# A scheduler that prices occupancy and latency apart, a gate whose left operands are turned by VectorE and by transfers, and operand tiles in three rooms

## The chip, the cores and the metric

The kernel runs on one core of one Trainium2 chip. A core has five engines with instruction queues of their own: TensorE (PE in the profile; its weight loads are PEld), VectorE (DVE), ScalarE (ACT), GpSimd (POOL) and SyncE (SP), which here only starts transfers. They meet through semaphores. The metric is the device time of one execution in microseconds (us). The time before is the median of three runs, 806.38 us, with 805.48 the lowest and 808.88 the highest.

## The reference, cut to what matters

One layer of a streaming encoder trunk is computed for 1024 prompt rows and 32 sample rows of width 1024, in float32:

```python
hn = rmsnorm(h, g_pre)
qA, kA, vA, gA, qB, kB, vB, gB = split(hn @ w_in)          # w_in: 1024 x 4096
oA = band_attention(qA, kA, vA)       # 8 heads x 64, own chunk of 64 and 8 before, biases
oB = stick_breaking(qB, kB, vB)       # 8 heads x 64, log-sigmoids and a reverse cumulative sum
y  = concat(oA * silu(gA), oB * silu(gB)) @ w_out           # 1024 x 1024
h  = h + rmsnorm(y, g_post)                                 # called h1 here
h  = h + sigmoid(h @ w_ple_gate) * (p @ w_ple)              # gate: 1024 x 1024
```

The outputs are h and the key and value caches. The change concerns the passage from the last line but one to the last: h1 stands with its rows on the partitions after the norm, and the gate's matmul wants it with its columns on the partitions.

## The kernel before, in words

**How precision is kept.** A float32 operand is split into a high part in a short float type (F32R) and a low remainder; a product is three matmuls, high by high, high by low and low by high (`multiply`, L1568). The high part is a ScalarE cast, the low part a VectorE subtraction.

**Stages.** From 0 to about 50 us the input rows are normed and turned and the first projections run. From 50 to about 550 us eight pairs of heads of the two attentions run, with the next pairs' input projections between them; about 550 to 605 us are the last input projection, 605 to 622 us the products `ple` of p. From 622 to 705 us runs the output projection ("o" in the names), from 705 to 801 us the gate projection ("g"), and the rest is the tail.

**The two last projections.** Both are Strassen-Winograd products over tiles of 128 rows. There are four sets: o with row tiles (0,4) and (1,5), o with (2,6) and (3,7), then g with the same two. A pair inside a set is an upper tile t and a lower tile t+4. Each set runs seven products in the order P1, P2, P6, P7, P4, P5, P3, and each product is 12 matmuls of 128x512 for each of the two pairs. In the profile the pair's products write tiles `o0P`, `o1P`, `g0P` and so on, after the upper row tile. The left operands A11, A12, S2, S3, A22, S1, S4 are made by `Side.make` (L1547) two or three products ahead (`AHEAD`): a ScalarE copy into PSUM, a ScalarE cast to the high part (`whA11o`, or a part of `A11o0`), a VectorE subtraction for the low part, and for some a GpSimd or VectorE combination before. `Side.room` gives them their places: pair 0 rotates over three rooms, two in the pool `fb` and one in `fa`, both tagged "ao"; pair 1 has `wpool` tiles. The short ninth tile (32 sample rows) has operands from `short_left` (L1642) and products from `short_product` (L1666); for the gate they are called `x8g`, `xb8g` and `g8`, and run after the third set.

**The gate's input.** `Row.close` (L1597) takes the mean square of a finished row tile, scales it by VectorE into `h1`, adds x by GpSimd and stores h1 to memory (`h_dr`). `Side.load` (L1530) makes the two operand tiles of a pair, `u` for tile t in pool `at2` and `l` for tile t+4 in pool `at0` or `fa`, and calls `fetch_T` (L1507) for each. For o it loads turned rows straight from memory. For g it loads the 128 rows of h1 in one transfer (`ht`), turns them by eight TensorE transposes into two PSUM banks (`pth`), and copies the banks to SBUF by two ScalarE copies (`ug`, `lg`). It does so for nine tiles. `Side.load` for the next set's pair is called when the last operand (n equal to 6) of this set's pair is made.

**What sets the order.** The body only records operations. `Recorder.order` (L372) is a list scheduler: each engine has a planned time at which it is free, an operation has a planned time at which its inputs are ready, and among the ready ones of an engine that with the smallest key goes first. The key is a class and the position in the program; `rec.low`, which is -2 or -1 around some row work, stands ahead of the position for the engines other than TensorE. `cost` (L338) gives two numbers: `busy`, how long the engine is taken, and `late`, how much later the result is there. In the kernel before only TensorE and the transfers have a `late` above 0. An operation on another engine is ready 60 ns after that (`SEM`), 460 ns if it is on TensorE (`MARGIN`); one on the same engine, when the engine is free. `emit` then issues all operations in the order found, each queue in turn, so the order is fixed before the kernel runs and every operation carries the line of `emit`, L450 in the profile. Instructions on a queue never pass each other. SP's queue holds all transfers.

Of the kernel before, what the change touches and what calls it, by code (L numbers as in the profile page):

```python
# [263 lines left out]
class Recorder:  # L264
# [73 lines left out]
    def cost(eng, method, args, kw, writes, reads):  # L338
# [8 lines left out]
        if eng == "ACT":  # L347
            return (165 if psum else 200) + 0.83 * n + (190 if "accum_out" in kw else 0), 0
        if eng == "DVE":
            if method == "tensor_tensor_scan":  # L350
                return 155 + 2.08 * n, 0
            if method == "tensor_copy" and not psum:
                return 155 + 0.53 * n, 0
            if method == "scalar_tensor_tensor":
                return 210 + 1.04 * n, 0
            return 155 + 1.04 * n + (83 if method == "tensor_tensor_reduce" else 0), 0
        if eng == "POOL":
            if method == "tensor_tensor":
                if n == 1:
                    return 400, 0  # L360
                return 190 + (1.77 if out.buf.dtype == F32 else 2.15) * n, 0
# [10 lines left out]
    def order(self):  # L372
# [17 lines left out]
        while len(out) < len(self.ops):  # L390
# [37 lines left out]
            for u in users[id(o)]:  # L428
                if u.eng == e and e != "SP":
                    r = t if e == "CTL" else free[e]  # L430
# [25 lines left out]
def stream_step(  # L456
# [1050 lines left out]
    def fetch_T(src, dst, t):  # L1507
# [5 lines left out]
        t0, n = rows_of(t)  # L1513
        h = fa.tile([P, D], F32, tag="hh", name=f"ht{t}", bufs=2)
        dma(h[0:n], h1_dr[t0:t0 + n, :])
        for q in range(2):
            pt = psum("T", f"pth{t}_{q}")
            for k in range(4):
                nc.tensor.transpose(pt[:, k * P:k * P + n], h[0:n, (q * 4 + k) * P:(q * 4 + k + 1) * P], ident[0:n, 0:n])
            nc.scalar.copy(dst[:, 4 * q:4 * q + 4, 0:n], pt.rearrange("p (k t) -> p k t", k=4)[:, :, 0:n])  # L1520


    class Side:
# [6 lines left out]
        def load(self):  # L1530
            self.u = at2.tile([P, KD, P], F32, tag="tok", name=f"u{self.nm}", bufs=2)
            if self.first:
                self.l = fa.tile([P, KD, P], F32, tag="hh", name=f"l{self.nm}", bufs=2)
            else:
                self.l = at0.tile([P, KD, P], F32, tag=("kd0", "kl0")[self.pair], name=f"l{self.nm}")
# [3 lines left out]
        def room(self, n, key):  # L1539
            if self.pair == 0:  # L1540
                one = Side.taken % 3 == 2
# [4 lines left out]

        def make(self, n, s2):  # L1547
            key = LEFT[ORDER[n]]
            u1, u2, l1, l2 = self.u[:, 0:4], self.u[:, 4:8], self.l[:, 0:4], self.l[:, 4:8]
# [7 lines left out]
            hi, lo = self.room(n, key)  # L1557
            beside = psum("mm" if self.m == 3 or (self.m == 2 and n > 1) else "T", f"x{key}{self.nm}").rearrange("p (k t) -> p k t", k=KT)
# [308 lines left out]
```

## Time and profile before

| | |
|---|---|
| median of the runs | 806.38 us (805.48 to 808.88, three runs) |
| the profiled execution, its own time | 808.3 us |
| its span, first to last instruction | 806.5 us |
| mean granted TensorE clock | 0.996 |
| TensorE busy in the span | 784.5 us, 97% |
| VectorE, ScalarE, GpSimd busy | 575.5, 507.8, 436.8 us |
| TensorE matmul records | 4646 |
| data moved by transfers | 161.08 MB |

The profile is of one execution; the 808.3 us are its time, 1.8 us longer than its span. A group line names an engine, an operation, the tile written and the tiles read, with the number of instructions. A waits line names what an engine waited for: the tile of the waiting instruction, the engine and the tile of what ended the wait, then the time in all, the number of waits and the longest one in us. A timeline line begins with the time in the span and the length in us; x12 means that twelve like instructions are drawn together, and the bracket at the end gives a wait before it. A windows line gives the stretch, its length, the busy time of PE, PEld, DVE, ACT and POOL with their counts, the granted clock, the transfers' share and GB/s. A tile answer gives line, engine, operation and tiles, the count, then the shortest, mean and longest duration in ns, the first and last start in us, and the shapes.

### The profile page before, as it was taken

To read this page: it belongs to the slowest core of one execution; us is meant where nothing else is said; L and a number is where in the kernel's file an instruction comes from. 1 tells how busy PE (TensorE), PEld (TensorE's weight loads), DVE (VectorE), ACT (ScalarE), POOL (GpSimd) and SP (SyncE) were. 2 spreads that over 40 slices of the span, in tenths; PEclk is the share of its full clock that TensorE was granted. 3 is DMA by queue.
4 is the path that set the end of the run, shared out by engine and by line. 5 is a ranking of instruction groups with operands and counts; after the bars stand their busy time and mean duration, and the time that the engine had idled before them with its cause. 6 is when DMAs were issued, how large, how long until landed. Compare 5 with 4: busy or idle time off the path is not lost.

```text
span 806.5 us, 14268 instructions
## 1 busy us (share of the span) xinstructions
PE 784.5 (97%) x4646; PEld 722.4 (90%) x4646; DVE 575.5 (71%) x1007; ACT 507.8 (63%) x1063; POOL 436.8 (54%) x503
## 2 busy tenths in 40 slices
PE   8999999999999999999999999999998999999997
PEld 6899989999889998999999989999996877888786
DVE  6627678886588897778896878766355687586565
ACT  5636675676476655785666685543337867876741
POOL 5613656873556676234660336777541537699523
PEclk9999999999999999999999999999999999999999
DMA  8419987668877749745545667774579767659743
GB/s 275 152 38 276 232 247 243 168 181 237 229 210 228 203 147 272 190 137 152 125 115 159 153 171 231 218 211 151 156 236 329 245 188 231 216 179 343 249 137 131
DMA packets 160971, 161.08 MB, mean 200 GB/s; under 512 B 39153, under 2 KB 120793, under 8 KB 160898
## 3 DMA queue, kind: packets, MB, share of 16 engines
q1 hardware_dynamic: 160898, 160.18, 67.0%
q8 instruction: 37, 0.61, 0.3%
q14 instruction: 36, 0.29, 0.1%
HBM read 99.23 MB, written 52.49 MB: 188 GB/s over the span
## 4 chain that ended last, share of the span: by engine, by line
PE 84%; ACT 5%; POOL 3%; DVE 3%; DMA 2%; issue 2%; SPq 1%; DVEq 0%; ACTq 0%; POOLq 0%
PE mm_gB L450 6%; PE mm_gA L450 6%; PE mm_qA L450 5%; PE mm_kA L450 5%; PE mm_vA L450 5%; PE mm_qB L450 4%; PE mm_kB L450 4%; PE SB L450 4%; PE PVB L450 4%; PE mm_vB L450 3%; PE PVA L450 3%; PE SA L450 3%; PE ptwB L450 3%; PE o0P L450 3%; PE o1P L450 2%; PE g0P L450 2%
## 5 line engine op out<-in xcount | busy, mean ns | idle before, releaser
L450 DVE TENSOR_TENSOR_SCAN om<-om,SB 128x384 f32<-128x384 f32 (+5 forms) x96 | 95.6, 1005 | 12.1 <-ACT om L450 9.8
L450 POOL TENSOR_TENSOR be<-om 128x128 f32<-128x128 f32 (+7 forms) x64 | 77.5, 1216 | 49.4 <-DVE om L450 23.1
L450 ACT ACTIVATE om<-SB 128x384 f32<-128x384 f32 (+5 forms) x96 | 44.9, 494 | 29.9 <-DVE SB L450 17.7
L450 ACT ACTIVATE be<-om,statA 128x640 f32<-128x640 f32 (+3 forms) x64 | 44.5, 696 | 12.1 <-DVE statA L450 6.9
L450 ACT CAST wTh<-ptwB 128x512 fp32r<-128x512 f32 (+3 forms) x64 | 29.4, 482 | 21.1 <-PE ptwB L450 16.2
L450 DVE TENSOR_TENSOR wTl<-be,wTh 128x640 fp32r<-128x640 f32 (+1 forms) x32 | 35.5, 1108 | 7.1 <-ACT wTh L450 6.8
L450 DVE TENSOR_TENSOR wTl<-ptwB,wTh 128x512 fp32r<-128x512 f32 (+3 forms) x64 | 33.5, 545 | 7.7 <-ACT wTh L450 4.6
L450 DVE TENSOR_TENSOR wTl<-ptwA,wTh 128x512 fp32r<-128x512 f32 (+2 forms) x64 | 29.8, 482 | 11.6 <-ACT wTh L450 10.1
L450 PE MATMUL SB<-kdB,LB 128*128 128x384 f32 (+5 forms) x96 | 33.7, 354 | 1.9 <-DVE om L450 1.9
L450 DVE CUSTOM_DVE_ANT_0 om<-SA,biasA 128x320 f32<-128x320 f32 (+3 forms) x64 | 30.0, 483 | 6.2 <-PE SA L450 5.8
L450 PE MATMUL SB<-klB,LB 128*128 128x384 f32 (+5 forms) x96 | 32.9, 347 | 0.0
L450 DVE STREAM_TRANSPOSE om<-be 128x640 f32<-128x640 f32 (+1 forms) x32 | 28.8, 900 | 4.7 <-ACT be L450 2.3
L450 ACT CAST wTh<-ptwA 128x512 fp32r<-128x512 f32 (+2 forms) x64 | 26.1, 424 | 9.0 <-PE ptwA L450 8.2
L450 PE MATMUL SA<-kdA,LA 128*128 128x320 f32 (+2 forms) x96 | 30.0, 322 | 1.3 <-DVE LA L450 0.7
L450 POOL TENSOR_TENSOR sggA<-sggA,oggA 128x352 f32<-128x352 f32 x24 | 23.9, 997 | 13.6 <-DVE sggA L450 10.2
L450 POOL TENSOR_TENSOR oB<-oB,oB 128x256 f32<-128x256 f32 x32 | 24.4, 783 | 12.0 <-DMA oB<-in_w_out_dram 5.8
L450 PE MATMUL SA<-klA,LA 128*128 128x320 f32 (+2 forms) x96 | 29.3, 316 | 0.0
L450 PE MATMUL ptwB<-ident,be 128*128 128x128 f32 x192 | 29.3, 273 | 0.0
L450 ACT CAST wTh<-be 128x640 fp32r<-128x640 f32 (+1 forms) x32 | 24.9, 779 | 6.4 <-DMA be<-swapA 3.8
L450 PE MATMUL ptwA<-ident,be 128*128 128x128 f32 x160 | 26.8, 274 | 2.0 <-ACT be L450 1.3
L450 POOL TENSOR_TENSOR gB<-gB,gB 128x256 f32<-128x256 f32 x32 | 24.3, 783 | 4.7 <-DMA gB<-in_w_ple_gate_dram 4.3
L450 DVE TENSOR_TENSOR SB<-SB,maskb 128x128 f32<-128x128 f32 x64 | 17.6, 290 | 11.3 <-PE SB L450 11.1
(707 smaller groups left out, 2659.7 us busy)
## 6 DMA issues: line engine op xcount, KB each, us to landing
swapA<-om SPq DMA_DIRECT2D x16, 320.0 KB, 2.7
be<-swapA SPq DMA_DIRECT2D x64, 80.0 KB, 3.2
oB<-in_w_out_dram SPq DMA_DIRECT2D x16, 256.0 KB, 4.6
sum_dro<-oB SPq DMA_DIRECT2D x16, 256.0 KB, 3.8
gB<-in_w_ple_gate_dram SPq DMA_DIRECT2D x16, 256.0 KB, 4.2
sum_drg<-gB SPq DMA_DIRECT2D x16, 256.0 KB, 3.0
x<-in_x_prompt_dram SPq DMA_DIRECT2D x16, 256.0 KB, 4.0
h_dr<-h SPq DMA_DIRECT2D x8, 512.0 KB, 3.2
```

The costliest lines, as they stand in the source:

```text
L450: getattr(getattr(tc.nc, o.what[0]), o.what[1])(*args, **kw)
```

## The change

**The planner's prices.** For ScalarE, VectorE and GpSimd's tensor operations the one price becomes two: a smaller time for which the engine is taken and a time (105, 85 or 150, and 40 ns) by which the result comes later. An operation that needs a result of its own engine is now ready when that result is there and not when the engine is free, except on TensorE. No instruction changes by this; the order in which each queue gets them does.

**The gate's input rows.** `Row.close` has a new step: VectorE transposes the finished 128x1024 row tile in squares of 32x32 into a tile `hs` (one buffer in `fb`), and a transfer stores it to memory as `turned` (512 KB). The plain store to `h_dr` stays, as the gate's last addition reads it. `fetch_T` for the gate has no TensorE transposes, no PSUM banks and no copies any more: four transfers, one for each quarter of the columns, read 32 partitions each of `turned` and so put the squares where they belong. In the operand tile a column's 128 rows then lie in four runs of 32 elements, so the operations of `make` read through a `blocks` view that puts them in order. In all 72 transposes and 18 copies go, nine VectorE transposes, nine stores and 36 loads in place of nine come.

**The rooms.** The operand tiles `u` and `l` of a pair now come from one of three rooms in rotation, (2m + pair) mod 3: two buffers "tok" in `at2`, two "hh" in `fa`, or "kd0"/"kl0" in `at0`. A pair's tiles are loaded three pairs ahead (`wanted`, `load_sides`), as soon as the room's former pair is done with its operands and, for the gate, the two row tiles are turned. In `Side.room` the pool `fa` gives the first of every three places and not the third, so the very first operand `A11o0` has its place in `fa`.

```diff
@@ -345,20 +345,22 @@
                 return (109 if args[1].shape[0] > 64 else 62), 165
             return max(109.0, 2.5 + 0.449 * args[2].free()) * (1 if args[2].buf.dtype == F32R else 4), 165
         if eng == "ACT":
-            return (165 if psum else 200) + 0.83 * n + (190 if "accum_out" in kw else 0), 0
+            return (60 if psum else 95) + 0.83 * n + (190 if "accum_out" in kw else 0), 105
         if eng == "DVE":
             if method == "tensor_tensor_scan":
-                return 155 + 2.08 * n, 0
+                return 120 + 2.1 * n, 85
             if method == "tensor_copy" and not psum:
-                return 155 + 0.53 * n, 0
+                return 70 + 0.53 * n, 85
             if method == "scalar_tensor_tensor":
-                return 210 + 1.04 * n, 0
-            return 155 + 1.04 * n + (83 if method == "tensor_tensor_reduce" else 0), 0
+                return 125 + 1.04 * n, 85
+            if method == "tensor_tensor_reduce":
+                return 90 + 1.04 * n, 150
+            return 70 + 1.04 * n, 85
         if eng == "POOL":
             if method == "tensor_tensor":
                 if n == 1:
-                    return 400, 0
-                return 190 + (1.77 if out.buf.dtype == F32 else 2.15) * n, 0
+                    return 535, 40
+                return 170 + (1.77 if out.buf.dtype == F32 else 2.15) * n, 40
             if method == "tensor_scalar":
                 return 255 + 0.86 * n, 0
             return 100 + 0.82 * n, 0
@@ -427,7 +429,7 @@
             out.append(o)
             for u in users[id(o)]:
                 if u.eng == e and e != "SP":
-                    r = t if e == "CTL" else free[e]
+                    r = t if e == "CTL" else free[e] if e == "PE" else done
                 else:
                     r = done + (0 if u.eng == "CTL" else SEM + (MARGIN if u.eng == "PE" else 0))
                 u.ready = max(u.ready, r)
@@ -1510,15 +1512,14 @@
             for k0 in (0, 4):
                 dma(dst[:, k0:k0 + 4, :], rows_T(og_dr, k0, t))
             return
-        t0, n = rows_of(t)
-        h = fa.tile([P, D], F32, tag="hh", name=f"ht{t}", bufs=2)
-        dma(h[0:n], h1_dr[t0:t0 + n, :])
-        for q in range(2):
-            pt = psum("T", f"pth{t}_{q}")
-            for k in range(4):
-                nc.tensor.transpose(pt[:, k * P:k * P + n], h[0:n, (q * 4 + k) * P:(q * 4 + k + 1) * P], ident[0:n, 0:n])
-            nc.scalar.copy(dst[:, 4 * q:4 * q + 4, 0:n], pt.rearrange("p (k t) -> p k t", k=4)[:, :, 0:n])
-
+        n = rows_of(t)[1]
+        G = n // 32
+        landed = dst.rearrange("p k t -> p (k t)")[:, 0:KD * n].rearrange("p (g x) -> p g x", g=G)
+        for c in range(4):
+            dma(landed[32 * c:32 * c + 32], turned[t][0:n, c * 256:(c + 1) * 256].rearrange("(g j) x -> j g x", j=32))
+
+
+    turned = {}
 
     class Side:
         taken = 0
@@ -1528,25 +1529,30 @@
             self.nm, self.src, self.t, self.pair, self.made = f"{nm}{t}", src, t, pair, {}
 
         def load(self):
-            self.u = at2.tile([P, KD, P], F32, tag="tok", name=f"u{self.nm}", bufs=2)
-            if self.first:
-                self.l = fa.tile([P, KD, P], F32, tag="hh", name=f"l{self.nm}", bufs=2)
-            else:
-                self.l = at0.tile([P, KD, P], F32, tag=("kd0", "kl0")[self.pair], name=f"l{self.nm}")
+            pool, tags, bufs = ((at2, ("tok", "tok"), 2), (fa, ("hh", "hh"), 2), (at0, ("kd0", "kl0"), 1))[(2 * self.m + self.pair) % 3]
+            self.u, self.l = (pool.tile([P, KD, P], F32, tag=tag, name=f"{x}{self.nm}", bufs=bufs) for x, tag in zip("ul", tags))
             fetch_T(self.src, self.u, self.t)
             fetch_T(self.src, self.l, self.t + 4)
 
         def room(self, n, key):
             if self.pair == 0:
-                one = Side.taken % 3 == 2
+                one = Side.taken % 3 == 0
                 Side.taken += 1
                 x = (fa if one else fb).tile([P, 2, KT, P], F32R, tag="ao", name=f"{key}{self.nm}", bufs=1 if one else 2)
                 return x[:, 0], x[:, 1]
             return [wpool.tile([P, KT, P], F32R, tag=tag, name=f"{tag}{key}{self.nm}", bufs=4) for tag in ("wh", "wl")]
 
+        def blocks(self, x):
+            if self.src is og_dr:
+                return x.rearrange("p k (g q) -> p k g q", q=32)
+            return x.rearrange("p k t -> p (k t)").rearrange("p (g k q) -> p k g q", g=4, q=32)
+
         def make(self, n, s2):
             key = LEFT[ORDER[n]]
-            u1, u2, l1, l2 = self.u[:, 0:4], self.u[:, 4:8], self.l[:, 0:4], self.l[:, 4:8]
+            u, l = (self.blocks(x) for x in (self.u, self.l))
+            u1, u2, l1, l2 = u[:, 0:4], u[:, 4:8], l[:, 0:4], l[:, 4:8]
+            if s2 is not None:
+                s2 = s2.rearrange("p k (g q) -> p k g q", q=32)
             if key == "S2":
                 if self.first:
                     nc.gpsimd.tensor_tensor(u1, u1, l1, ALU.subtract)
@@ -1554,8 +1560,9 @@
             if key == "S4":
                 nc.gpsimd.tensor_tensor(u2, u2, s2, ALU.subtract)
             x = {"A11": u1, "A12": u2, "S2": s2, "S3": u1, "A22": l2, "S1": l1, "S4": u2}[key]
-            hi, lo = self.room(n, key)
-            beside = psum("mm" if self.m == 3 or (self.m == 2 and n > 1) else "T", f"x{key}{self.nm}").rearrange("p (k t) -> p k t", k=KT)
+            made = self.room(n, key)
+            hi, lo = (z.rearrange("p k (g q) -> p k g q", q=32) for z in made)
+            beside = psum("mm" if self.m == 3 or (self.m == 2 and n > 1) else "T", f"x{key}{self.nm}").rearrange("p (k g q) -> p k g q", k=KT, q=32)
             nc.scalar.copy(beside, x)
             nc.scalar.copy(hi, x)
             nc.vector.tensor_tensor(lo, beside, f(hi), ALU.subtract)
@@ -1563,7 +1570,7 @@
                 nc.vector.tensor_tensor(u1, beside, l1, ALU.subtract)
             if key == "A22":
                 nc.vector.tensor_tensor(l1, beside, l1, ALU.add)
-            self.made[n] = (hi, lo)
+            self.made[n] = made
 
     def multiply(acc, left, b, cols):
         hi, lo = left
@@ -1605,8 +1612,15 @@
                 nc.vector.scalar_tensor_tensor(h, h, r[0:n], g_banks[q][0:n], ALU.mult, ALU.mult)
                 rec.low = -1
                 nc.gpsimd.tensor_tensor(h, h, self.x[q][0:n], ALU.add)
+            rec.low = -2
+            turned[self.t] = scratch([P, D], f"turned{self.t}")
+            x = fb.tile([P, D], F32, tag="hs", name=f"hs{self.t}")
+            nc.vector.transpose(x[0:n].rearrange("p (c b q) -> p b c q", c=4, q=32), self.h1[0:n])
+            dma(turned[self.t][0:n], x[0:n])
+            rec.low = -1
             dma(h1_dr[self.t0:self.t0 + n, :], self.h1[0:n])
             rec.low = 0
+            load_sides()
 
     def h1_room(i, t):
         if i == 2:
@@ -1685,6 +1699,17 @@
     sides = [[Side(nm, src, t, i, m) for i, t in enumerate(g)] for m, (nm, src, g) in enumerate(sets)]
     s2s = {}
 
+    wanted = [0, 1, 2]
+
+    def load_sides():
+        for i in list(wanted):
+            if i >= 2 * len(sets):
+                continue
+            side = sides[i // 2][i % 2]
+            if side.src is og_dr or {side.t, side.t + 4} <= set(turned):
+                wanted.remove(i)
+                side.load()
+
     def prepare_left(step, pair):
 
         m, n = divmod(step, 7)
@@ -1693,14 +1718,14 @@
         if m not in s2s and LEFT[ORDER[n]] == "S2":
             s2s[m] = at0.tile([P, 2, KT, P], F32, tag="v20", name=f"s2_{m}")
         sides[m][pair].make(n, s2s[m][:, pair] if m in s2s else None)
-        if n == 6 and m + 1 < len(sets):
-            sides[m + 1][pair].load()
+        if n == 6:
+            wanted.append(2 * m + pair + 3)
+            load_sides()
 
     for q in range(2):
         g_banks.append(psum("mm", f"g_post{q}"))
         nc.scalar.copy(g_banks[q], GP[:, HALF[q]])
-    for pair in range(2):
-        sides[0][pair].load()
+    load_sides()
     for n in range(3):
         for pair in range(2):
             if n < AHEAD[pair]:
```

## The prediction, made before the changed kernel was run

> **What bounds the kernel now.** I read the page first, then the waits of TensorE, then the windows by stage, then the timeline at the two places where TensorE stands still longest, and at last the tiles that the change touches.
>
> ```profile
> span 806.5 us, 14268 instructions
> PE 784.5 (97%) x4646; PEld 722.4 (90%) x4646; DVE 575.5 (71%) x1007; ACT 507.8 (63%) x1063; POOL 436.8 (54%) x503
> ```
>
> TensorE is busy 784.5 of 806.5 us; no other engine comes near. So a matmul that goes is worth its own time, and everything else counts only where TensorE waits for it. The view of waits says where that is (rows that the argument does not use are left out):
>
> ```profile
> PE o0P L450 <- ACT A11o L450: 2.5, 1, 2.5
> PE ptx L450 <- DVE be L450: 2.2, 2, 1.3
> PE SB L450 <- DVE om L450: 1.9, 3, 1.1
> PE mm_kB L450 <- ACT stvA L450: 1.5, 1, 1.5
> PE PVA L450 <- ACT wTh L450: 1.3, 1, 1.3
> PE ptwA L450 <- ACT be L450: 1.3, 1, 1.3
> ...
> PE ptsA L450 <- DVE sumsA L450: 1.0, 2, 0.9
> ...
> PE SA L450 <- DVE statA L450: 0.6, 1, 0.6
> PE ptwA L450 <- DVE wTl L450: 0.4, 2, 0.2
> ...
> PE ptwA L450 <- ACT ktB L450: 0.3, 1, 0.3
> PE PVsA L450 <- DVE otA L450: 0.2, 1, 0.2
> PE ptkB L450 <- ACT sumrowA L450: 0.2, 1, 0.2
> ```
>
> All of these but the first two lie in the attentions: short waits, none above 1.5 us, for a result of ScalarE or VectorE that stood too late in its queue. The windows of the two output stages show a different picture:
>
> ```profile
> 600.00:650.00 50.00, 47.50 (x212) 38.64 (x211) 30.76 (x51) 39.04 (x80) 15.52 (x12) 0.97 0.84 267
> 650.00:700.00 50.00, 50.00 (x233) 39.45 (x232) 35.45 (x55) 37.20 (x79) 32.25 (x37) 1.00 0.72 231
> 700.00:750.00 50.00, 50.00 (x234) 40.90 (x233) 37.15 (x60) 35.86 (x75) 43.42 (x42) 1.00 0.73 246
> ```
>
> From 650 us TensorE has no gap at all, and VectorE is free for 14.6 and 12.9 us of each 50. The one gap is at the start of the output projection, and it is also where the granted clock falls, to 0.97 over the 50 us:
>
> ```profile
> 621.89 0.99 PE L450 MATMUL o0P<-oB,A11o 128*128 128x512 f32 x2 [2.50 <-ACT A11o L450]
> 623.54 3.42 PE L450 MATMUL o0P<-oB,A11o 128*128 128x512 f32 x10
> 626.80 0.40 PE L450 MATMUL o1P<-oB,wlA11o 128*128 128x512 f32 x1
> 629.10 2.90 PE L450 MATMUL o0P<-oB,A12o 128*128 128x512 f32 x12
> ```
>
> After 2.50 us of standing still the next matmuls take 0.99/2 and 3.42/10 us each, where later ones take 2.90/12 = 0.24. That is 0.5 + 1.0 + 0.2 = 1.7 us of half speed behind a wait of 2.5: together 4.2 us. The waits of 1.3 to 1.5 us above have no such stretch behind them.
>
> **The transposes that go.**
>
> ```profile
> L450 PE MATMUL pth<-ident,ht x72: 220/272/273, 688.9 to 759.5; 128*128 128x128 f32 x64, 32*128 32x32 f32 x8
> 746.44 1.03 PE L450 MATMUL pth<-ident,ht 128*128 128x128 f32 x8
> 747.23 1.17 PE L450 MATMUL g0P<-gB,S4g 128*128 128x512 f32 x4
> ```
>
> The next matmul starts 747.23 − 746.44 = 0.79 us after the first of eight transposes, so a tile costs 0.79 us of TensorE; the 272 ns of a single one overlap. Eight tiles give 6.3, the short one (eight of 32x32) some 0.5: −6.8 us. They lie at 688.9 to 759.5, where TensorE has no gap, so all of it is on the path. The 18 ScalarE copies that go were beside other work and bring nothing directly.
>
> **The new step and its transfers.** The nearest rows are a VectorE square transpose of the same shape and the transfers of the same size:
>
> ```profile
> L450 DVE STREAM_TRANSPOSE vxB<-stvB x4: 1221/1238/1249, 123.2 to 484.6; 128x1024 f32<-128x1024 f32 x4
> h_dr<-h SPq DMA_DIRECT2D x8, 512.0 KB, 3.2
> be<-swapA SPq DMA_DIRECT2D x64, 80.0 KB, 3.2
> ```
>
> Eight full tiles at 1.24 and a short one are some 10 us of VectorE between about 650 and 715 us, against the 27 us that it has free in 650 to 750: hidden. If that cover were gone, as where a subtraction that TensorE waits for stands right behind a transpose, one costs up to 1.24 us. On SP's queue nine stores (3.2 us each to landing) and 27 more issues are added, and each load stands behind what the planner put ahead of it there. The loads have 3.2 us too by the nearest row, and operands are now asked for three pairs ahead. I find from the order of the queues that the time from an operand's load to its first product has little slack from 606 to 705 us, above all in the first two g sets. Bounds: nothing, if transfers keep to 3.2 us; +11 us (worked out as a rival below), if each new link adds its full price. Nearer to nothing, by the free time of VectorE: +1. Less than nothing is possible only through the copies gone from ScalarE, which is busy 36 of 50 us there and is what TensorE waits for nowhere after 650.
>
> **The operands read in runs of 32.** The operations of `make` keep their sizes. No row shows such a pattern priced against a plain one for these operations; a 32-square transpose reads and writes so at 1238 ns for 1024 elements, near the plain rate (0.69 us for 512, below). I take nothing, and at most some 0.1 us for each of seven operands, off the path.
>
> **The start of the output projection.** `A11o0` now has its place in `fa`, free early, so it no longer waits for a room that the last split of a weight block holds. In the order after, TensorE runs P1 and P2 of pair 0 and then P1 of pair 1 (`o1P`), whose high part, the cast `whA11o`, stands on ScalarE behind the square of the first h1 half. That square needs the sum of P2, so it cannot begin before pair 0's second product has ended:
>
> ```profile
> 798.24 0.69 DVE L450 TENSOR_TENSOR uu<-uu,g2P 128x512 f32<-128x512 f32 x1
> L450 ACT ACTIVATE junk<-h x16: 587/602/622, 632.8 to 712.8; 128x512 f32<-128x512 f32 x16
> L450 ACT ACTIVATION_READ_ACCUMULATOR junk<-h x16: 185/187/202, 633.3 to 713.3; 128x1 f32 x16
> L450 ACT CAST whA11o<-uo x2: 610/616/622, 618.6 to 656.6; 128x512 fp32r<-128x512 f32 x2
> ```
>
> With the VectorE sum of that size from the tail at 0.69 us: 0.69 + 0.60 + 0.19 + 0.62 = 2.1 us of a new standstill in place of 2.5. If the half-speed stretch follows here as well (1.7), the place costs 3.8 in place of 4.2: −0.4.
>
> **The short tile of the gate.** Before, its operands were ready early:
>
> ```profile
> L450 DVE TENSOR_TENSOR x8g<-xb8g,x8g x3: 273/274/293, 730.2 to 734.6; 128x128 fp32r<-128x128 f32 x2, 128x128 f32<-128x128 f32 x1
> L450 ACT CAST x8g<-xb8g x2: 255/258/261, 733.5 to 733.7; 128x128 fp32r<-128x128 f32 x2
> L450 ACT COPY xb8g<-x8g x1: 378/378/378, 729.8 to 729.8; 128x256 f32<-128x256 f32 x1
> L450 PE MATMUL g<-gB,x8g x24: 387/392/473, 753.1 to 760.1; 128*64 128x512 f32 x24
> 798.96 0.60 ACT L450 ACTIVATE sg<-uu 128x512 f32<-128x512 f32 x1 [1.59 <-DVE uu L450]
> ```
>
> The last operand was written near 735, its products began at 753.1. After, the four loads of this tile stand late on SP's queue, and the planner puts `xb8g` on ScalarE behind the sigmoid of the third set's last product (`sg`), while TensorE's queue has the products `g8` right behind that very product. So from its end TensorE waits for: sum 0.69, the multiplication that frees the one sigmoid bank 0.69 (the same shape), sigmoid 0.60, then 0.38 + 0.26 + 0.27 + 0.26 + 0.27. That is 3.4 us, with 1.7 of half speed 5.1: +5.1. What comes in g's fourth set only moves behind it. Bounds: 2.9, if the second low part is not waited for with the first matmul, and 5.6.
>
> **The attentions.** The planner's order alone changes here. A wait that comes from a result standing too late in a queue can go when the planner knows that a result comes 105 or 85 ns after the engine is free; one that comes with a table load or a transfer cannot:
>
> ```profile
> 470.75 1.28 ACT L450 ACT_TABLE_LOAD   x1
> 473.83 0.66 PE L450 MATMUL ptwA<-ident,be 128*128 128x128 f32 x4 [1.31 <-ACT be L450]
> ```
>
> Here a load of tables of 1.28 us stands ahead of `be`, and TensorE waits 1.31; loads stand so ahead of the waits of 1.5 and 1.3 (`mm_kB`, `PVA`) too, and the transitions that call for them are as many after. Of the others, 1.9 + 1.0 + 0.6 + 0.4 + 0.3 + 0.2 + 0.2 = 4.6 us, the queues after show slack at all of them. I take −4.6; bounds 0 (each wait comes back elsewhere) and −8.7 (with the three that hang on table loads). The start, where `ptx` waits 2.2 us in two waits, gets other neighbours: −0.5, bounds 0 and −2.2.
>
> **The sum** is made against the profiled execution, whose span of 806.5 us happens to stand 0.1 above the median of the runs, 806.38; its own time, 808.3, is 1.9 above it, and the difference of spans is carried to the median: −6.8 + 1.0 − 0.4 + 5.1 − 4.6 − 0.5 = −6.2, so 806.4 − 6.2 = 800.2 us. About 0.5%, 4 us, is what a measurement of this kernel can tell from no change: faster is below 802.4, slower above 810.4.
>
> **The rivals.** First: no half-speed stretch follows either new standstill. The row says that 2.5 us sufficed and that 1.5 did not; 2.1 lies between. Then both places are 1.7 less: 800.2 − 3.4 = 796.8. For it: the three waits of 1.3 to 1.5 us had none; against it: the only single wait above 2 us had one.
>
> The Trainium skill, "TensorE: Matmul & The Clock Gate", section "Part 1: The HAM clock gate", says that the clock goes to half after an idle window of about 3.4 us. By that rule the 2.1 us at the start of the projection would bring none, and the 3.4 us at the short tile would be on its edge; the trace differs, with half speed after 2.5 us. By the rule the time would be that of this rival.
>
> Second: the attentions give nothing. An order by other prices moves every queue, and what goes in one place comes back in another. For it: the short waits are spread over 500 us, each with its own cause; against it: the new prices sum to nearly the same latency, and the queues show slack at those seven. 800.2 + 4.6 = 804.8, the same as before.
>
> Third, and slower: the single buffer `hs`. Each transpose waits for the store of the one before, 3.2 us to landing, with 1.24 of its own 4.4 us per tile, against 2.8 us per product of TensorE. Were the rows to come one after the other at each product and all VectorE work behind be held, 1.6 us would be lost seven times, 11.4 in all (to the digit that the rows give): 800.2 + 11.4 = 811.6. It decides when a store lands 3 us or more after its transpose and a subtraction that TensorE needs stands next in VectorE's queue. Against it: 5 to 13 VectorE instructions stand between two transposes in the order.
>
> **How the numbers follow.** The forecast 0.42; no half speed 0.20; attentions without gain 0.26; the buffer 0.10; 0.02 for other. The range goes from 795.5, the first rival with a part of the start's waits too, to 808.5, the second with some of the gate's queues. The likeliest case alone spans 798 to 802.4. Faster 0.60 (forecast and first rival less their edge), same 0.29, slower 0.11.
>
> **What would show it.** In the changed kernel: 4574 TensorE records, no `pth`, and 6.8 us less TensorE time; a wait of `o1P` for `whA11o` near 2.1 us and one of `g8` for `x8g` near 3.4, with slow matmuls behind or not; the seven attention waits missing; `hs` transposes of 1.24 us with waits for the store that TensorE does not feel. The prediction is wrong if operands of the gate (`A11g`, `S2g`) come to stand in the waits of TensorE after 650 us, or new waits above 1 us stand in the attentions.

## The result: 1% slower, and the profile after

The changed kernel takes 813.83 us (median of six runs, 812.52 to 819.08) beside 805.99 us for the kernel before on the same chip; the ratio is 1.0101, with a 95% interval of 1.0080 to 1.0122. The forecast was 800.2 us and its range ended at 808.5. The profiled execution took 812.52 us with a span of 810.5, 4.0 us above the span before. The profiled execution before took 808.3 us, 2.3 above its kernel's median, and the one after is the fastest of its six, so this pair of profiles shows some 4 of the 7.8 us between the medians; the account by stages below covers these 4, and what makes the rest is not shown.

The first lines of the page of the changed kernel:

```profile
span 810.5 us, 14177 instructions
PE 784.0 (97%) x4574; PEld 716.1 (88%) x4574; DVE 578.7 (71%) x1016; ACT 498.3 (61%) x1043; POOL 432.4 (53%) x503
```

The 72 transposes are gone (4646 to 4574 records), yet the span is longer, so TensorE stands still, or runs at half speed, more than it did. (In the changed kernel every operation carries L452, in kernels with the old prices L450.) The longest of its waits after the change (in all, times, longest, in us):

```profile
PE g L452 <- DVE x8g L452: 3.6, 1, 3.6
PE o1P L452 <- ACT whA11o L452: 2.4, 1, 2.4
PE g1P L452 <- ACT whA11g L452: 1.9, 1, 1.9
PE ptwA L452 <- ACT be L452: 1.8, 2, 1.3
PE SB L452 <- DVE om L452: 1.6, 3, 0.9
...
PE ptkA L452 <- DVE wTl L452: 1.3, 1, 1.3
PE o3P L452 <- DVE h L452: 1.3, 1, 1.3
PE ptwA L452 <- DVE wTl L452: 1.0, 1, 1.0
PE g0P L452 <- ACT A11g L452: 0.8, 1, 0.8
...
PE g0P L452 <- DVE A11g L452: 0.8, 1, 0.8
```

The first two were forecast. The third and the two for A11g were not: they stand at the start of the gate projection. The prediction had named just this, operands of the gate among the waits after 650 us, as a sign that it is wrong, and new waits above 1 us in the attentions as another; `ptkA` for `wTl` (1.3) is one of these. The windows show the gate's waits, and two stretches with the clock at 0.97 where there were none before (columns as in the windows quoted in the prediction):

```profile
650.00:700.00 50.00, 48.55 (x211) 37.41 (x210) 38.35 (x56) 33.95 (x69) 36.58 (x40) 1.00 0.82 250
700.00:750.00 50.00, 46.45 (x192) 36.50 (x191) 38.17 (x56) 29.50 (x57) 37.92 (x39) 0.97 0.95 301
750.00:800.00 50.00, 46.44 (x194) 34.90 (x193) 28.91 (x49) 24.36 (x47) 17.19 (x14) 0.97 0.47 147
```

ScalarE is busy 29.5 us of 700 to 750 where it was busy 35.9: it is not overloaded, it waits. The transfers' share there rises from 0.73 to 0.95.

To see where the time went I took, for each two matmuls that follow each other, the distance between their starts less the pace of the first one's shape at full speed (0.232 us for 512 columns, 0.109 for 128), and summed it by stage. It holds standstill and half speed together; where packed matmuls go a little faster than the pace, a sum is slightly negative.

| us lost by TensorE in | 0 to 50 | 50 to 600 | 600 to 650 | 650 to 700 | 700 to 750 | 750 to 800 | sum |
|---|---|---|---|---|---|---|---|
| before | 6.8 | 9.5 | 4.4 | −0.4 | 0.0 | −0.4 | 20.0 |
| after | 5.8 | 9.1 | 3.9 | 1.5 | 6.0 | 5.4 | 31.7 |

The records that are gone take 7.5 us of pace with them; 11.7 us are lost instead, 11.7 less 7.5 is the 4 us of the span. Of the 11.7, some 5.8 are the short tile, which was forecast, 6.0 the start of the gate and 1.9 the stage before it, which were not; up to 600 us 1.4 is won where 5.1 had been forecast, and 0.5 at the start of the output projection.

### The profile page after: what moved, and what is told of

It is laid out like the page before. It is cut to its first block, busy times and chain, and to the rows that moved or that the text cites. A ratio compares the mean times of both kernels' runs of the same rounds, so it can differ in the third digit from the quotient of the medians.

```text
span 810.5 us, 14177 instructions
## 1 busy us (share of the span) xinstructions
PE 784.0 (97%) x4574; PEld 716.1 (88%) x4574; DVE 578.7 (71%) x1016; ACT 498.3 (61%) x1043; POOL 432.4 (53%) x503
## 4 chain that ended last, share of the span: by engine, by line
PE 65%; DMA 6%; ACT 6%; DVE 4%; issue 3%; POOL 2%; SPq 1%; ACTq 0%; DVEq 0%; POOLq 0%
PE mm_gA L452 6%; PE mm_gB L452 6%; PE mm_kA L452 4%; PE mm_vA L452 4%; PE PVB L452 4%; PE mm_qA L452 4%; PE SB L452 4%; PE mm_qB L452 3%; PE mm_kB L452 3%; PE g1P L452 3%; PE mm_vB L452 2%; DMA raw<-sum_drg 2%; PE g2P L452 2%; PE ptwB L452 2%; PE g3P L452 2%
## 5 line engine op out<-in xcount | busy, mean ns | idle before, releaser
L452 POOL TENSOR_TENSOR be<-om 128x128 f32<-128x128 f32 (+7 forms) x64 | 75.5, 1185 | 63.7 <-DVE om L452 31.3
L452 DVE TENSOR_TENSOR_SCAN om<-om,SB 128x384 f32<-128x384 f32 (+5 forms) x96 | 95.0, 1001 | 9.6 <-ACT om L452 7.9
L452 ACT ACTIVATE om<-SB 128x384 f32<-128x384 f32 (+5 forms) x96 | 44.4, 493 | 37.0 <-DVE SB L452 27.9
L452 ACT ACTIVATE be<-om,statA 128x640 f32<-128x640 f32 (+3 forms) x64 | 44.4, 695 | 18.2 <-DVE statA L452 11.1
L452 DVE TENSOR_TENSOR wTl<-be,wTh 128x640 fp32r<-128x640 f32 (+1 forms) x32 | 38.2, 1194 | 8.5 <-ACT wTh L452 6.7
L452 DVE TENSOR_TENSOR wTl<-ptwB,wTh 128x512 fp32r<-128x512 f32 (+3 forms) x64 | 33.7, 546 | 11.2 <-ACT wTh L452 8.6
L452 ACT CAST wTh<-ptwB 128x512 fp32r<-128x512 f32 (+3 forms) x64 | 29.5, 481 | 19.3 <-PE ptwB L452 15.1
L452 DVE TENSOR_TENSOR wTl<-ptwA,wTh 128x512 fp32r<-128x512 f32 (+2 forms) x64 | 29.8, 483 | 15.6 <-ACT wTh L452 12.5
L452 POOL TENSOR_TENSOR oB<-oB,oB 128x256 f32<-128x256 f32 x32 | 27.4, 875 | 18.5 <-DMA oB<-in_w_out_dram 9.7
L452 DVE STREAM_TRANSPOSE om<-be 128x640 f32<-128x640 f32 (+1 forms) x32 | 28.9, 904 | 9.8 <-POOL be L452 5.1
L452 PE MATMUL SB<-kdB,LB 128*128 128x384 f32 (+5 forms) x96 | 34.3, 359 | 1.6 <-DVE om L452 1.6
L452 ACT CAST wTh<-ptwA 128x512 fp32r<-128x512 f32 (+2 forms) x64 | 26.1, 425 | 13.2 <-PE ptwA L452 7.5
L452 DVE CUSTOM_DVE_ANT_0 om<-SA,biasA 128x320 f32<-128x320 f32 (+3 forms) x64 | 29.5, 482 | 6.2 <-PE SA L452 4.8
L452 PE MATMUL SB<-klB,LB 128*128 128x384 f32 (+5 forms) x96 | 32.9, 345 | 0.0
L452 PE MATMUL SA<-kdA,LA 128*128 128x320 f32 (+2 forms) x96 | 30.0, 323 | 0.6 <-DVE LA L452 0.4
L452 POOL TENSOR_TENSOR sggA<-sggA,oggA 128x352 f32<-128x352 f32 x24 | 23.9, 994 | 11.2 <-DVE sggA L452 10.8
L452 PE MATMUL SA<-klA,LA 128*128 128x320 f32 (+2 forms) x96 | 29.6, 320 | 0.0
L452 PE MATMUL ptwA<-ident,be 128*128 128x128 f32 x160 | 26.5, 276 | 3.0 <-ACT be L452 1.8
L452 PE MATMUL ptwB<-ident,be 128*128 128x128 f32 x192 | 28.8, 273 | 0.0
L452 ACT CAST wTh<-be 128x640 fp32r<-128x640 f32 (+1 forms) x32 | 25.0, 782 | 4.9 <-DMA be<-swapA 3.2
L452 DVE TENSOR_TENSOR SB<-SB,maskb 128x128 f32<-128x128 f32 x64 | 17.3, 288 | 11.6 <-PE SB L452 11.4
L452 POOL TENSOR_TENSOR klA<-stkA,kdA 64x1024 fp32r<-64x1024 f32 x8 | 20.8, 2596 | 8.2 <-ACT kdA L452 7.7
```

The source lines that it names most:

```text
L452: getattr(getattr(tc.nc, o.what[0]), o.what[1])(*args, **kw)
```

## The experiments

All times are medians of repeated runs beside the kernel before on the same chip, unless a single execution is named; the interval is that of the ratio, and us lost by TensorE are those of the one profiled execution. I began with three theories. A: the gate's operand loads are planned one behind the other. B: the planner's prices spoil the order of the output stage. C: the added transfers land late because the queue is full.

**The planner alone.** The kernel before, with the price and rule hunks of the change and nothing else.

```diff
-            return (165 if psum else 200) + 0.83 * n + (190 if "accum_out" in kw else 0), 0
+            return (60 if psum else 95) + 0.83 * n + (190 if "accum_out" in kw else 0), 105
...
-                    r = t if e == "CTL" else free[e]
+                    r = t if e == "CTL" else free[e] if e == "PE" else done
```

> The kernel before with the planner's new prices alone: the gate's rows are still turned by TensorE, the rooms are the old ones. Theory A (the time was lost in the gate's operand loads, and the attentions simply gained almost nothing): 805 to 807 us, TensorE's waits before 600 us some 0.5 us less in all than the 15 us before, no long wait after 650 us. Theory B (the new prices make the order of the output stage worse): 809 us or more, with waits above 1 us after 650 us. The forecast on record for this part alone was 806.0 - 5.1 = 801 us.

Measured: 809.28 us beside 806.95, ratio 1.0026 (1.0006 to 1.0046). Its waits:

```profile
PE PVA L452 <- ACT wTh L452: 3.2, 1, 3.2
PE o0P L452 <- ACT A11o L452: 2.3, 1, 2.3
PE ptwA L452 <- ACT be L452: 1.8, 2, 1.3
PE SB L452 <- DVE om L452: 1.6, 3, 0.9
PE ptkA L452 <- DVE wTl L452: 1.5, 1, 1.5
```

The time is neither theory's by itself: A put 805 to 807 us here, and B's 809 or more is reached. But B's sign, waits above 1 us after 650 us, is not there; what TensorE loses from 650 to 800 us is 0.9 us in all, beside −0.8 before, so some 1.7 us are lost in the output stage in this execution, in no long wait. Nor do the attentions gain: the waits of 1.0 for `sumsA` and 0.6 for `statA` are no longer among these, and `ptkA` for `wTl` (1.5) and a longer `PVA` come in their place. The planner's half of the change, forecast at −5.1 us, costs 2.3.

**The quarter loads seen as four regions.** A rearranged view in this recorder forgets which axis is which, so a slice of it counts as the whole tile. The four loads of an operand write four separate quarters of the partitions, but the planner takes each as a second write of the same tile and plans it behind the landing of the one before. Slicing first gives it the true regions:

```diff
-        landed = dst.rearrange("p k t -> p (k t)")[:, 0:KD * n].rearrange("p (g x) -> p g x", g=G)
         for c in range(4):
-            dma(landed[32 * c:32 * c + 32], turned[t]...)
+            landed = dst[32 * c:32 * c + 32].rearrange("p k t -> p (k t)")[:, 0:KD * n].rearrange("p (g x) -> p g x", g=G)
+            dma(landed, turned[t]...)
```

In the changed kernel's timeline the four loads of the short tile, its first use on ScalarE and its first product stand so:

```profile
733.04 1.06 SPq L452 DMA_DIRECT2D x8g<-turned  x1
738.53 0.43 SPq L452 DMA_DIRECT2D x8g<-turned  x1
744.29 0.48 SPq L452 DMA_DIRECT2D x8g<-turned  x1
750.01 0.42 SPq L452 DMA_DIRECT2D x8g<-turned  x1
755.31 0.36 ACT L452 COPY xb8g<-x8g 128x256 f32<-128x256 f32 x1
756.97 3.28 PE L452 MATMUL g<-gB,x8g 128*64 128x512 f32 x10 [3.56 <-DVE x8g L452]
```

From the first issue to the last it is 17 us, though each lands in 3.7 us by the view of transfers:

```profile
x8g<-turned SPq DMA_DIRECT2D x4, 32.0 KB, 3.7
```

At the gate's start the same holds for `ug`: the eight quarters for the first two pairs go out one by one from 687.05 to 708.20 (with separate quarters, from 689.93 to 699.69), and the product of the second pair, which needs all four of its own, stands still until 715.78.

```profile
708.20 0.41 SPq L452 DMA_DIRECT2D ug<-turned  x1
713.91 0.58 ACT L452 COPY xA11g<-ug 128x512 f32<-128x512 f32 x1
715.78 0.73 PE L452 MATMUL g1P<-gB,whA11g 128*128 128x512 f32 x2 [1.94 <-ACT whA11g L452]
```

> The changed kernel, with the four quarter loads of a gate operand sliced by partitions before they are rearranged, so that the planner's own bookkeeping sees four separate regions and not the whole tile four times; the instructions are the same, only their order and the waits differ. Theory A (the four loads are planned one behind the other's landing, so that an operand is complete about 20 us after its first load; that makes the gate's first products and its short tile late): the waits for A11g, whA11g and x8g (0.8 + 0.8 + 1.9 + 3.6 us, with half speed about 11) go, 801 to 805 us. Theory B (planner's prices) and theory C (more transfers on a full queue land late): 811 to 814 us, as the traffic and the prices are the same.

Measured: 811.42 us, ratio 1.0051 (1.0029 to 1.0073). The four loads now go out together, and the waits for `x8g` and `A11g` are gone, as A has it, but a new one takes much of the gain:

```profile
740.06 2.23 SPq L452 DMA_DIRECT2D x8g<-turned  x4
```

```profile
PE g1P L452 <- DVE uu L452: 3.9, 1, 3.9
```

The time is near the bound that B and C gave, the place is not: so A was right about these waits and wrong about the time, and something else stood behind them. TensorE loses 8.6 us from 700 to 750 and nothing more after 750.

**Old prices, without and with separate quarters.** The changed kernel with the planner hunks taken back, and the same with the quarters separate.

> The changed kernel with the planner's old prices and rule: turned rows and rooms alone. Theory A: the operand loads are still in a row, so the waits at the gate's start and its short tile stay, 812 to 816 us. Theory B: these waits go, 800 to 805 us. Theory C: 812 to 816 us, too.

> Turned rows, rooms, quarter loads seen as separate, old prices. Theory A: near the kernel with separate quarters and new prices, 801 to 806 us; what differs between the two is what the planner's prices are worth by themselves, within 1 us by the first of these runs. Theory B: 800 to 805 us, as without separate quarters. Theory C: 811 to 815 us.

Measured: 813.21 us, ratio 1.0078 (1.0053 to 1.0103), with these waits:

```profile
PE g L450 <- DVE x8g L450: 3.1, 1, 3.1
PE g0P L450 <- ACT A11g L450: 3.0, 1, 3.0
PE g1P L450 <- ACT whA11g L450: 2.3, 1, 2.3
```

And with separate quarters 810.27 us, ratio 1.0037 (1.0016 to 1.0058), with these gone and this one in their place:

```profile
PE g1P L450 <- DVE uu L450: 5.8, 1, 5.8
```

This is above the 801 to 806 us that A gave, for the same reason as in the run before. The gate's waits come with the quarters planned in a row at either prices, so B does not explain them; and as the traffic is the same in the changed kernel and in these three, C does not either. The two halves of the change, each alone, cost 2.3 us (the planner) and 6.3 us (rows and rooms, at old prices); together they cost 7.8.

**The place of the sums.** `uu` is a tile of the gate's sums; it takes one of three rooms "stg" in turn, and the turn gives it the room of row 2's `h1`, which was taken first. Row 2 is turned third of its set. In the kernel with separate quarters VectorE's timeline reads:

```profile
717.35 1.25 DVE L452 STREAM_TRANSPOSE hs<-h 128x1024 f32<-128x1024 f32 x1
...
726.02 1.23 DVE L452 STREAM_TRANSPOSE hs<-h 128x1024 f32<-128x1024 f32 x1
...
734.04 1.24 DVE L452 STREAM_TRANSPOSE hs<-h 128x1024 f32<-128x1024 f32 x1
735.21 0.65 DVE L452 TENSOR_TENSOR uu<-p1g,g0P 128x512 f32<-128x512 f32 x1
```

The rows are turned 8.0 to 8.7 us apart: 1.2 us of transpose, up to 1.4 us until the store's turn on SP's queue, some 5 us to landing, and other work of VectorE up to the next transpose. That the one buffer `hs` sets this spacing, by the order that the planner makes of it, is argued: these two transposes do not wait for the buffer in the trace, and no run gave `hs` a second one. The sum that gives a PSUM bank back starts right after the third. So rows 6 and 7 were given their rooms before row 2; `uu` then follows row 6, which is turned first.

```diff
+                if m == 1 and (prod, pair) == ("P1", 0):
+                    for i, x in enumerate(group):
+                        state[i]["h1l"] = h1_room(2 * i + 1, x + 4)
                 if nm == "o" and prod == "P7":
-                    st["h1l"] = h1_room(2 * pair + 1, t + 4)
+                    if m == 0:
+                        st["h1l"] = h1_room(2 * pair + 1, t + 4)
```

> Separate quarter loads, and besides the h1 tiles of rows 6 and 7 take their places in the ring of three before row 2's, so that the gate's sums (uu) of its first pair get the place of row 6, which is turned first, and not that of row 2, which is turned third. Theory D (with one hs buffer the rows are turned some 8.5 us apart, and uu waits for the place of the row that is turned third): the 3.9 us wait of g1P for uu and the half speed around it go, 804 to 807 us. Rival (the third standstill has another cause, an addition that stands too late in VectorE's queue): the wait stays, 810 to 812 us.

> The same with the planner's old prices. Theory D: the 5.8 us wait of g1P for uu goes, 802 to 806 us. If the planner's new prices are worth nothing or cost something, as the run of these prices alone says, this one is not slower than the one with new prices; if they help the output stage, it is 1 us or more slower.

> The changed kernel with rows 6 and 7 first, but the quarter loads still in a row. Theory A says that the loads alone hold the gate's start and its short tile here: no gain, 812 to 815 us. If the place of uu were the whole cause, 806 to 808 us.

Measured: with new prices 806.00 us, ratio 0.9990 (0.9977 to 1.0003); with old prices 807.45, ratio 1.0022 (1.0004 to 1.0041); without separate quarters 813.43, ratio 1.0087 (1.0056 to 1.0119). In the first the sum no longer waits for the third transpose:

```profile
726.63 1.23 DVE L452 STREAM_TRANSPOSE hs<-h 128x1024 f32<-128x1024 f32 x1
730.16 0.67 DVE L452 TENSOR_TENSOR uu<-p1g,g0P 128x512 f32<-128x512 f32 x1
...
735.10 1.23 DVE L452 STREAM_TRANSPOSE hs<-h 128x1024 f32<-128x1024 f32 x1
```

So the late room was the cause of the wait for `uu`, as theory D has it, and the order of the two causes is shown too: while the loads are late, the room costs nothing that these runs can tell (ratio 1.0087 beside 1.0101, with intervals that overlap). The kernel with old prices lies above its expectation of 802 to 806; two waits of 2.4 (`g3P`) and 1.9 us (`S2g`) have come in place of the one for `uu`. It is also 1.4 us slower than the one with new prices on the same chip, and from 700 to 800 us TensorE loses some 7 us in it beside 3: by the expectation the new prices do help the output stage once the loads and the room are mended, though alone they cost 2.3 us and, with separate quarters only, no difference between old and new shows (810.27 and 811.42, with intervals that overlap).

**The start of the output projection.** Two edits were made on this kernel: the first two pairs' tiles `u` back in `tok`, and the first operand's place back in `fb`.

```diff
-            pool, tags, bufs = ((at2, ("tok", "tok"), 2), (fa, ("hh", "hh"), 2), (at0, ("kd0", "kl0"), 1))[(2 * self.m + self.pair) % 3]
+            pool, tags, bufs = ((at2, fa), ("tok", "hh"), 2) if (2 * self.m + self.pair) % 3 < 2 else ((at0, at0), ("kd0", "kl0"), 1)
```

```diff
-                one = Side.taken % 3 == 0
+                one = Side.taken % 3 == 2
```

> Separate quarter loads, rows 6 and 7 first, and the operand rooms so that each of the first two pairs has its tile u in tok and its tile l in hh, as before the change, with the third room as changed. Theory E (the 2.4 us wait of o1P for whA11o comes from the second pair's u, which now has its place in a pool that opens late): the wait goes, 802 to 805 us. Rival (the wait comes from the order of the loads and of ScalarE's queue): it stays near 2.4 us, 805 to 807 us.

> Separate quarter loads, rows 6 and 7 first, and the pool fa gives the third of every three operand places, as before the change, and not the first. If the room of the first operand A11o0 is what made TensorE wait 2.5 us before, the wait of o0P for A11o is back here (2.3 to 2.8 us) and that of o1P for whA11o is gone: the same time within 1 us as with the new place, 804 to 807 us. If both waits stand, 807 us or more.

> The kernel of the look at the first operand's room, timed: separate quarter loads, rows 6 and 7 first, the third operand place in fa. The look at it had 802.3 us, 21.6 us of standstill and half speed in all beside 25.7 with the first place in fa. If that is the order's doing and not the execution's, 803 to 805 us and faster than before by 0.2 to 0.5%; if it was one good execution, 805.5 to 807 us.

> The same, and besides the operand rooms of the first two pairs as before the change (u in tok, l in hh). The waits at the start of the output projection did not come from these rooms, so this is within 1 us of the kernel without it: 803 to 806 us.

Measured: `u` in `tok` 805.91 us, ratio 0.9985 (0.9962 to 1.0007), with the wait of `o1P` unchanged at 2.4 us, so theory E is out. The first operand's place: a single execution of 802.29 us, then twelve of the same kernel with a median of 804.61, ratio 0.9973 (0.9958 to 0.9988); both edits together 805.44, ratio 0.9982 (0.9962 to 1.0001). With the old place the wait of `o0P` for `A11o` is back and that of `o1P` is gone, as expected: the place moves the standstill, it does not remove it. What the place is worth by itself is not shown, as the intervals with the old place and with the new one (0.9977 to 1.0003) overlap. The kernel with separate quarters, rows 6 and 7 first and the old place is the one that beats the kernel before, by 0.27%.

The single execution and the profile of the repeated runs, of one kernel on two chips, also show the same wait with two different sequels. In the single execution:

```profile
619.57 4.45 PE L452 MATMUL o0P<-oB,A11o 128*128 128x512 f32 x12 [2.33 <-ACT A11o L452]
```

and in the profile of the repeated runs:

```profile
620.48 3.28 PE L452 MATMUL o0P<-oB,A11o 128*128 128x512 f32 x12 [2.34 <-ACT A11o L452]
```

**The rule without the latencies it carries.** New prices, but a dependent operation of the same engine is ready when the engine is free, on the kernel with separate quarters, rows 6 and 7 first and `u` in `tok`.

> The same with the planner's new prices but its old rule, by which a dependent operation of the same engine is ready when the engine is free. It leaves the added latency out for chains within an engine. If the rule is what keeps the attentions' waits down at the new prices, the waits between 200 and 240 us and 450 to 470 us return and the time is 3 to 8 us above the kernel with the rule, 808 to 813 us; if the rule does nothing, both are within 1 us.

Measured: 820.77 us, ratio 1.0142 (1.0098 to 1.0186), 14.9 us above the same kernel with the rule (805.91) and well above the 808 to 813 expected. TensorE loses 41.8 us in place of 23.0, most of it from 200 to 600 us (some 16 us more) and from 750 to 800 (some 7 more); from 100 to 200 us it loses some 4 us less. Three of its waits:

```profile
PE g3P L452 <- ACT whA11g L452: 3.1, 1, 3.1
PE o3P L452 <- DVE h L452: 2.5, 2, 1.5
PE mm_kB L452 <- ACT stvA L452: 2.3, 1, 2.3
```

So the order is worth a great deal, and the rule is needed with the smaller prices; with both, put on the kernel before, the time is 0.26% above that with the old ones.

## Why the prediction was wrong, step by step

On the pair of profiles the account gives some +4 us where −6.2 was forecast. Two terms make the difference: the new step with its transfers, too low by 6.9 us, and the attentions, by 4.2; the others miss by 0.7 at most and nearly cancel.

**The transposes (−6.8)** were right: 72 records less, and with them 7.5 us of pace off TensorE's path.

**The new step and its transfers (+1.0, bounds 0 and 11)** is the step that failed most. It took each load at the 3.2 us of the nearest row and leaned to nothing because VectorE had room, though it had found little slack between an operand's load and its first product. What it cost is 1.9 us from 650 to 700 and 6.0 from 700 to 750, 7.9 in place of 1.0. The four quarters of an operand are planned one behind the other, so that an operand is complete some 20 us after its first load and not 5. The order that I had read showed the four loads of the short tile far apart on SP's queue; I read it as "late", and did not ask why four loads that need nothing from each other do not stand together. Separate quarters and the room of `uu` take most of the cost away: from 700 to 750 TensorE loses 2.3 us in the kernel with both, and 1.5 in the single execution of the one that beats the kernel before.

**The transfers' own time** was mis-sized as well. The stores of `turned` land in 4.4 us and the quarters in 5.3 to 5.5, and other loads land later; here is one kind of them before and after, in the view of transfers from 640 to 800 us (size, then us to landing):

```profile
raw<-sum_drg SPq DMA_DIRECT2D x16, 256.0 KB, 3.8
```

```profile
raw<-sum_drg SPq DMA_DIRECT2D x16, 256.0 KB, 7.0
```

The amount alone does not explain it: with the planner alone, without a byte more, these loads take 5.5 us, and in the kernel with old prices, separate quarters and rows 6 and 7 first, with all the added traffic, 3.5:

```profile
raw<-sum_drg SPq DMA_DIRECT2D x16, 256.0 KB, 5.5
```

```profile
raw<-sum_drg SPq DMA_DIRECT2D x16, 256.0 KB, 3.5
```

At equal traffic, separate quarters alone bring it from 7.0 to 5.3 us at new prices and from 6.1 to 3.3 at old ones. So the order moves it; that it is what stands together on the queue is argued and not shown. The kernels with separate quarters carry the same traffic without the gate's first waits.

**The short tile (+5.1)** came as forecast: a wait of 3.56 us for `x8g`, half speed behind it, 5.8 us in all with the small gain of the stage before. The chain that I had worked out to 3.4 us is the one in the trace. Its cause was missed: it goes with separate quarters.

**The start (−0.5)** was about right and **the attentions (−4.6)** were wrong. In the pair of profiles TensorE loses 6.8 us up to 50 us before and 5.8 after, and from 50 to 600 us 9.5 before and 9.1 after. Over all the profiles here that use the prices and rule of the change (nine executions) the means are 5.6 and 10.3 us, over those with the old ones (four executions) 6.5 and 9.4: the start wins 0.9 and the attentions lose it again. From 200 to 250 us 4.6 to 4.7 us become 1.0 to 2.0, as forecast; from 100 to 200 us 1.5 to 3.6 become 3.6 to 6.3. That is the second rival, which had 0.26: what goes in one place comes back in another. The traces show what is the order's in this. In the nine every engine and SP's queue have one and the same order up to 607 us, in the four the old one up to 590. The waits of `mm_kB` for `stvA` (1.5 to 1.6 us) and of `ptsA` for `sumsA` (0.9 to 1.0) stand in all four and in none of the nine; the wait of `ptkA` for `wTl` (1.3 to 1.5, near 150 us) stands in all nine and in none of the four. Of the waits that were to go, the largest, `SB` for `om` (1.9), is still 1.6 in the changed kernel, and `ptwA` for `wTl` grew from 0.4 to 1.0; one that was to stay, `mm_kB` behind its table load, went. The rest is the execution's: the wait of `PVA` for `wTh` near 102 us goes from 0.4 to 3.2 us among executions of the same order. Why the new order makes `ptkA` wait is not settled.

**The start of the output projection (−0.4)** came out at −0.5, by other terms: the standstills are 2.4 and 0.5 us and no half speed follows them in this execution. That the sum comes out so near is luck: the 2.4 us follow the forecast chain of 2.1, but of the five profiles with this very wait three have half speed behind it.

**The slower rival (single `hs`, 811.6 us)** had the right part and the wrong way. VectorE stands 3.1 us for the buffer in all, and the wait of `o3P` for `h` (1.3) stands behind one of these; but what cost most is that `h1` gives its room back late, which showed only after the loads were mended (3.9 and 5.8 us). That its 811.6 us lie nearer to the measured time than the forecast is chance.

**Half speed after a standstill.** The prediction set a threshold somewhere between 1.5 and 2.5 us. There is none to be seen: over the 14 profiled executions a standstill after the first 50 us, measured as the distance of starts beyond the pace, was followed within 8 us by at least five half-speed matmuls in 3 of 43 cases from 1.3 to 1.8 us, 2 of 7 from 1.9 to 2.2, 11 of 14 from 2.4 to 2.8 and 8 of 8 above 3. The Trainium skill, "TensorE: Matmul & The Clock Gate", section "Part 1: The HAM clock gate", says that the clock falls after an idle window of some 3.4 us, and that the window runs freely, so that the same kernel differs from run to run. The second half fits the two sequels of one wait shown above; the first does not, since 2.3 us sufficed often and 1.5 us now and then. The record of the granted clock in these traces has 24 stretches of half speed from 50 to 800 us, and each is 3.41 us long; TensorE loses 1.4 to 1.8 us in one, 1.6 in the mean. A standstill so costs its length and a chance of about 1.6 us more.

## What to carry to other kernels

When one transfer becomes four, look at where the four stand in the queue of the changed program: if they are spaced by more than a landing time (here 5.5 to 5.8 us with 3.7 to landing), the program may believe that they depend on each other, and its bookkeeping of regions is the first thing to read. A tile that is held longer than before delays whoever gets its room next, so for each room in rotation name the next taker and when the holder lets go. New prices for a planner change all orders at once; a gain read from waits that vanish is not a gain until the waits that appear have been counted over the same stretch.

## What the runs showed of the hardware that was not expected

The same standstill of 2.3 us is followed by half speed in one execution (4.45 us for twelve matmuls) and not in another (3.28 us), on another chip, of one and the same kernel. And the time to landing of one kind of load, 256 KB each, went from 3.8 to 7.0 us with the change, but to 5.5 by a new order alone and to 3.5 with the added transfers in another order: it follows the order of the program more than the bytes. Half speed, where it came between 50 and 800 us, lasted 3.41 us in all 24 cases.
